# Hyena layer: low parts by accumulating transfers and VectorE in place of GpSimd, spectrum products in four wide operations

## The chip, the core and the metric

One core of a Trainium2 chip runs two transformer blocks over 256 positions of width 1024. The metric is the device time of one execution in microseconds. TensorE (PE; PEld is its weight load), VectorE (DVE), ScalarE (ACT), GpSimd (POOL) and SyncE (SP, which issues most transfers) each take their own instructions in order and wait for each other by semaphores.

## The reference

The whole program is a first block (stick-breaking attention, memory attention, an FFN), an MLA layer with a convolutional FFN, and a Hyena layer with a convolutional FFN. The change is in the Hyena layer:

```python
def hyena_mixer(x, w_in, w_short, ..., d_bias, w_o):
    u = dwconv_centred(x @ w_in, w_short)          # 256 x 3072
    v, g1, g2 = jnp.split(u, 3, axis=-1)
    filt = hyena_filters(length, ...)
    n = 2 * length
    z = v
    for o, gate in enumerate((g1, g2)):
        k_f = jnp.fft.rfft(two_sided_kernel(filt[:, o, 0], filt[:, o, 1]), n=n, axis=0)
        z_f = jnp.fft.rfft(z, n=n, axis=1)
        y = jnp.fft.irfft(z_f * k_f, n=n, axis=1)[:, :length]
        z = gate * (y + d_bias[o] * z)
    return z @ w_o
```

Around it stand a layer norm and the FFN `(silu(g) * a) @ w_down` with `a, g = split(dwconv(x @ w_up))`.

## The kernel before

Every product is made of three matmuls on numbers split in two: `hi` is the value rounded to the short format that TensorE takes at full rate, `lo` is the rest, and hi·hi + lo·hi + hi·lo is summed in PSUM. A weight comes in slabs of 128 x 1024 floats (512 KB). `weights` loads a slab into `wraw` (3 buffers, by SP), ScalarE rounds it to `whi`, and another engine makes `wlo = wraw - whi` (`whi` and `wlo` have 5 buffers each). TensorE then takes, for a projection (`gemm_b`), eight products with whi, eight with wlo and eight with whi against the low part of x.

`share["every"]` says which engine makes `wlo`: with 0 it is VectorE, with n every n-th slab goes to GpSimd. In the Hyena layer's input projection it is `HY_POOL = 1`, so all 20 slabs (called 4 to 23; the first four come in another form) go to GpSimd, and for the 8 slabs of its output projection it is `WO_POOL = 2`, so four of them do.

The Hyena layer runs on TensorE in one written order. `hy_mm(nt)` projects slab nt into a bank `hin` (4 banks, shared with the `y` of the inverse transforms); `dwconv` makes `u` or `g` of it in three operations (ScalarE, then VectorE lines 761 and 763), which frees the bank; `hy_time` transposes two u into `hyt`. The 1024 channels are worked in two halves, and each half has two orders, so there are four spectra:
- `spectrum` multiplies z by the DFT matrices (`X`: 12 matmuls), ScalarE copies one half (`ev`), VectorE adds and subtracts into `W`, and then the complex product with the filter's spectrum `Kf` is made in ten VectorE operations of 128 x 512 and two additions on GpSimd (lines 954 to 959). Tiles are `spec_w` and `spec_q`.
- `even_odd` or `both` splits the result into `yh`, `yl`; `back1` or `back2` transforms back on TensorE into `y` and multiplies by the gate.
- Between a spectrum and its inverse, TensorE has projections of later slabs to do. For the fourth spectrum these are the first four slabs of the output projection (`acc`).

A scheduler in the tile layer sets each engine's order from dependences and its own cost estimates, so that the code's order is kept only roughly on VectorE and ScalarE; the order after the change is read from the built program below.

Of the kernel before, what the change touches and what calls it, by code (L numbers as in the profile page):

```python
# [9 lines left out]
F32 = mybir.dt.float32  # L10
# [3 lines left out]
AF = mybir.ActivationFunctionType  # L14
ALU = mybir.AluOpType
# [19 lines left out]
PI_IN = 3.1415925  # L35
RAW_BUFS = 3
SPLIT_BUFS = 5
HY_POOL = 1
WO_POOL = 2
FF2_POOL = (0, 0)  # L40
WARM = 12
F4_TAGS = (("f4h0", "f4l0"), ("f4h1", "f4l1"))

# [2 lines left out]
def block_kernel(ctx, tc, A, out, taps=None):  # L46
    nc = tc.nc
# [17 lines left out]
        return [[acc_bank(b, h) for h in range(2)] for b in range(2)]  # L65


    def split(hi, lo, src, eng=nc.vector):
        nc.scalar.activation(hi, src, AF.Copy)  # L69
        eng.tensor_tensor(lo, src, hi.bitcast(F32), op=ALU.subtract)  # L70
# [4 lines left out]
    def raw_tile():  # L75
        return wraw.tile([P, 1024], F32, name="wraw", tag="wraw")

    share = {"every": 0, "n": 0}

    def weights(ap, dst=None):  # L80

        share["n"] += 1
        eng = nc.gpsimd if share["every"] and share["n"] % share["every"] == 0 else nc.vector
        n = ap.shape[-1]
        raw = raw_tile()
        hi, lo = dst or [wspl.tile([P, 1024], F32R, name=t, tag=t) for t in ("whi", "wlo")]
        norm["load"] = nc.sync.dma_start(raw[:, :n], ap)
        with ExitStack() as es:
            if norm["after"] > 0:
                norm["after"] -= 1  # L90
                es.enter_context(tc.issue_after(norm["inst"].ins))
            split(hi[:, :n], lo[:, :n], raw[:, :n], eng)
        return hi, lo

    def gemm_b(ps, w, off, x, kts):
# [108 lines left out]
    class Down:  # L204
# [4 lines left out]
        def __init__(self, total, tail=TAIL):  # L209
            self.acc, self.n, self.head, self.pend = None, 0, total - tail, []  # L210

        def add(self, act, wap):
            w = weights(wap)
            if self.acc is None:
                self.acc = acc_banks()
            if self.n >= self.head:
                self.pend.append((act, w))
            else:
                for b in range(2):
                    for h in range(2):  # L220
                        gemm_a(self.acc, b, h, act, w, self.n == 0, False)
            self.n += 1
# [261 lines left out]
    dn = Down(8)  # L484
# [29 lines left out]
    dn = Down(FF1_TILES)  # L514
# [137 lines left out]
    for i in range(2):  # L652
        w = weights(A["w_uq_r"][i])
# [83 lines left out]
    dn = Down(8)  # L737
# [30 lines left out]
    Kf = keep.tile([P, 2, 2, 2, D], F32, name="Kf")  # L768
# [71 lines left out]
    def conv_ffn(layer, x, utok, nxt, side):  # L840
        with ExitStack() as es:
            pf = es.enter_context(tc.tile_pool(name=f"pf{layer}", bufs=1))
            todo = side(es.enter_context(tc.tile_pool(name="flt", bufs=1))) if side else []
            per = -(-len(todo) // (FF2_TILES - 5))
            wc = lnp.tile([P, 2 * FF2_TILES, 3], F32, name="wc", tag="wc")
            nc.sync.dma_start(wc, A["ffn_w_conv"][layer])
            gb = ln_load(pf, A["ln2_g"][layer], A["ln2_b"][layer])
            dn = Down(FF2_TILES, TAIL if nxt is not None else SPLIT_BUFS)
            share["every"] = FF2_POOL[layer]

            def mm(nt):
                w = weights(A["ffn_w_up"][layer, nt])
                ps = bank("up")
                gemm_b(ps[:, :S], w, 0, x, KT)
                return ps[:, :S]

            def act(j, pss):
                ts = []
                for i in range(2):
                    t = pf.tile([P, S], F32, name=f"t{i}", tag=f"t{i}", bufs=2)  # L860
                    dwconv(t, pss[i], wc[:, j + i * FF2_TILES, :])
                    ts.append(t)
                ta, tg = ts
                nc.scalar.activation(tg, tg, AF.Silu)
                nc.vector.tensor_tensor(ta, ta, tg, op=ALU.mult)
                return act_split(pf, ta, "h", 5)

            def up(j):
                return act(j, [mm(2 * (j - 2) + i) for i in range(2)])

            ready = [up(2)]
            ready += [act(j, first_pair(utok, j)) for j in range(2)]
            order = [2, 0, 1] + list(range(3, FF2_TILES))
            for i in range(FF2_TILES):
                if i + 3 < FF2_TILES:
                    ready.append(up(i + 3))
                dn.add(ready[i], A["ffn_w_down"][layer, order[i]])
                if i:
                    for f, *a in todo[(i - 1) * per:i * per]:
                        f(*a)  # L880
            share["every"] = 0
            return dn.end(gb, ALPHA_2, nxt)

    x, utok = conv_ffn(0, x, utok, A["hy_w_in_f"], hyena_filter)
# [8 lines left out]
    g2 = p4.tile([P, KT, S], F32, name="g2", tag="g2")  # L893

    def hy_mm(nt):
        w = weights(A["hy_w_in"][nt - 4])
        ps = bank("hin")
        gemm_b(ps[:, :S], w, 0, x, KT)
        return ps[:, :S]
# [36 lines left out]
    def spectrum(o, c, z, own):  # L936

        cs = slice(c * 512, (c + 1) * 512)
        fh, fl = dft["c_fwd"]
        W = p4.tile([P, 2, 2, 512], F32, name="spec_w", tag="spec_w")  # L940
        Q = p4.tile([P, 2, 2, 512], F32, name="spec_q", tag="spec_q")
        for j in range(2):
            eo = []
            for b in range(2):
                ps = acc_bank(j, b, "X") if own else bank("X")
                mm3(ps, (fh[:, b, j], fl[:, b, j]), (z[0][:, b], z[1][:, b]), True, True)
                eo.append(ps)
            ev = p4.tile([P, 512], F32, name="ev", tag="ev", bufs=2)
            nc.scalar.activation(ev, eo[0], AF.Copy)
            for i, op in enumerate((ALU.add, ALU.subtract)):  # L950
                nc.vector.tensor_tensor(W[:, i, j], ev, eo[1], op=op)
        for i in range(2):
            kr, ki = Kf[:, o, i, 0, cs], Kf[:, o, i, 1, cs]
            nc.vector.tensor_tensor(Q[:, i, 0], W[:, i, 0], kr, op=ALU.mult)
            nc.vector.tensor_tensor(Q[:, i, 1], W[:, i, 1], ki, op=ALU.mult)  # L955
            nc.vector.tensor_tensor(Q[:, i, 0], Q[:, i, 0], Q[:, i, 1], op=ALU.subtract)  # L956
# [86 lines left out]
    z0 = back1(0, y)  # L1043
# [150 lines left out]
```

## Time and profile before

| | |
|---|---|
| median of 3 runs | 989.87 us (989.59, 989.87, 994.86) |
| the profiled execution | 988.41 us, its span 986.6 us |
| mean granted TensorE clock in it | 0.986 |
| TensorE, VectorE, ScalarE, GpSimd busy | 946.4, 760.4, 524.5, 123.3 us |
| Hyena layer, first slab's projection to the last inverse | 644.9 to 773.4 us |

A row of the profile's groups names line, engine, operation, output<-inputs, shape and count, then busy time and mean duration in ns, then the idle time before it and what ended that. A row of the timeline is start, length, engine, line and tiles; `xN` at its end merges N neighbours. A row of waits reads: who waited for whom, total us, times, longest. The granted clock (PEclk) is the share of full speed that TensorE was given.

### The profile page before, as it was taken

To read this page: it belongs to the slowest core of one execution; us is meant where nothing else is said; L and a number is where in the kernel's file an instruction comes from. 1 tells how busy PE (TensorE), PEld (TensorE's weight loads), DVE (VectorE), ACT (ScalarE), POOL (GpSimd) and SP (SyncE) were. 2 spreads that over 40 slices of the span, in tenths; PEclk is the share of its full clock that TensorE was granted. 3 is DMA by queue.
4 is the path that set the end of the run, shared out by engine and by line. 5 is a ranking of instruction groups with operands and counts; after the bars stand their busy time and mean duration, and the time that the engine had idled before them with its cause. 6 is when DMAs were issued, how large, how long until landed. Compare 5 with 4: busy or idle time off the path is not lost.

```text
span 986.6 us, 15543 instructions
## 1 busy us (share of the span) xinstructions
PE 946.4 (96%) x6020; PEld 841.1 (85%) x6020; DVE 760.4 (77%) x1177; ACT 524.5 (53%) x859; POOL 123.3 (12%) x78
## 2 busy tenths in 40 slices
PE   9999999999999999999999999998879899999996
PEld 7889789888998888888899999788867789999995
DVE  6776678666557777779889887869998778777776
ACT  5676526445445576556666665345453346555551
POOL 0000000000000110011311211177453000000000
PEclk9999999999999999999999999999999899999999
DMA  7744436656565543466545556443222455555551
GB/s 242 278 170 129 154 122 221 178 190 179 183 192 187 173 128 107 149 244 210 196 164 184 171 170 220 132 160 106 98 86 86 171 192 193 179 185 185 181 191 43
DMA packets 48921, 165.97 MB, mean 168 GB/s; under 512 B 5995, under 2 KB 6860, under 8 KB 48720
## 3 DMA queue, kind: packets, MB, share of 16 engines
q1 hardware_dynamic: 48656, 164.34, 50.5%
q8 instruction: 47, 0.77, 0.3%
q0 software_dynamic: 192, 0.66, 0.2%
q14 instruction: 26, 0.21, 0.1%
HBM read 163.27 MB, written 1.05 MB: 167 GB/s over the span
## 4 chain that ended last, share of the span: by engine, by line
PE 76%; DVE 13%; DMA 5%; ACT 3%; issue 2%; POOL 0%; SPq 0%; DVEq 0%; ACTq 0%
PE up L102 30%; PE acc L108 8%; PE acc L107 8%; PE acc L109 8%; PE f L189 5%; PE proj L102 2%; DVE wlo L70 2%; PE z L107 1%; DMA wraw<-w_qk 1%; DVE yl L70 1%; DVE spec_q L956 1%; ACT whi L69 1%; DVE spec_q L955 1%; PE qn L102 1%; DMA wraw<-w_v 1%
## 5 line engine op out<-in xcount | busy, mean ns | idle before, releaser
L70 DVE TENSOR_TENSOR wlo<-wraw,whi 128x1024 fp32r<-128x1024 f32 (+1 forms) x246 | 300.6, 1225 | 71.2 <-ACT whi L69 70.9
L69 ACT ACTIVATE whi<-wraw 128x1024 fp32r<-128x1024 f32 (+1 forms) x270 | 281.0, 1045 | 113.3 <-PE acc L108 54.3
L102 PE MATMUL up<-xh,whi 128*128 128x256 f32 x864 | 122.0, 283 | 1.3 <-DVE t L763 1.3
L102 PEld LDWEIGHTS up<-xh,whi 128*128 128x128 f32 x864 | 115.3, 191 | 8.3 <-ACT whi L69 1.6
L102 PE MATMUL up<-xh,wlo 128*128 128x256 f32 x864 | 121.3, 283 | 0.0
L102 PE MATMUL up<-xl,whi 128*128 128x256 f32 x864 | 121.3, 283 | 0.0
L108 PE MATMUL acc<-whi,hl 128*128 128x512 f32 x304 | 119.6, 394 | 1.5 <-DVE hl L70 1.5
L109 PE MATMUL acc<-wlo,hh 128*128 128x512 f32 x304 | 119.6, 395 | 0.0
L107 PE MATMUL acc<-whi,hh 128*128 128x512 f32 x304 | 119.3, 394 | 0.0
L102 PEld LDWEIGHTS up<-xl,whi 128*128 128x128 f32 x864 | 111.5, 192 | 0.0
L102 PEld LDWEIGHTS up<-xh,wlo 128*128 128x128 f32 x864 | 111.4, 192 | 0.0
L156 POOL TENSOR_TENSOR ln_rs<-ln_rs,mhalf 128x1 f32<-128x1 f32 x12 | 11.7, 971 | 629.1 <-DVE ln_rs L155 629.1
L760 ACT ACTIVATE t<-up,wc 128x256 f32<-128x256 f32 x80 | 37.8, 474 | 94.8 <-PE up L102 94.7
L761 DVE SCALAR_TENSOR_TENSOR t<-up,wc,t 128x255 f32<-128x255 f32 x80 | 38.2, 479 | 51.4 <-ACT t L760 51.3
L108 PEld LDWEIGHTS acc<-whi,hl 128*128 128x128 f32 x304 | 57.1, 188 | 12.9 <-DVE hl L70 2.5
L109 PEld LDWEIGHTS acc<-wlo,hh 128*128 128x128 f32 x304 | 57.1, 188 | 12.7
L107 PEld LDWEIGHTS acc<-whi,hh 128*128 128x128 f32 x304 | 57.6, 189 | 10.9 <-ACT hh L69 0.6
L70 POOL TENSOR_TENSOR wlo<-wraw,whi 128x1024 fp32r<-128x1024 f32 x24 | 59.5, 2497 | 54.8 <-ACT whi L69 54.7
L763 DVE SCALAR_TENSOR_TENSOR t<-up,wc,t 128x255 f32<-128x255 f32 x80 | 38.3, 480 | 2.1
L524 ACT ACTIVATE h<-up 128x256 f32<-128x256 f32 x28 | 10.8, 385 | 54.7 <-PE up L102 51.5
L525 DVE TENSOR_TENSOR h<-h 128x256 f32<-128x256 f32 x32 | 13.5, 424 | 27.0 <-ACT h L524 26.4
L829 POOL TENSOR_TENSOR Kf<-f_eo 128x512 f32<-128x512 f32 x16 | 23.0, 1460 | 63.5 <-ACT f_eo L826 63.5
(411 smaller groups left out, 1684.6 us busy)
## 6 DMA issues: line engine op xcount, KB each, us to landing
wraw<-ffn_w_up SPq DMA_DIRECT2D x80, 512.0 KB, 3.5
wraw<-ffn_w_down SPq DMA_DIRECT2D x44, 512.0 KB, 3.5
wraw<-w_down SPq DMA_DIRECT2D x32, 512.0 KB, 3.7
wraw<-w_up SPq DMA_DIRECT2D x28, 512.0 KB, 3.6
wraw<-hy_w_in SPq DMA_DIRECT2D x20, 512.0 KB, 3.3
wraw<-w_qk SPq DMA_DIRECT2D x14, 512.0 KB, 4.6
wraw<-w_out SPq DMA_DIRECT2D x8, 512.0 KB, 3.5
wraw<-mla_w_o SPq DMA_DIRECT2D x8, 512.0 KB, 3.3
```

Of the source, the lines that this page charges most:

```text
L69: nc.scalar.activation(hi, src, AF.Copy)
L70: eng.tensor_tensor(lo, src, hi.bitcast(F32), op=ALU.subtract)
L102: nc.tensor.matmul(ps, a[:, off + k * P:off + (k + 1) * P], m[:, k, :], start=i == 0, stop=i == len(seq) - 1)
L107: nc.tensor.matmul(ps, ah, mh, start=start, stop=False)
L108: nc.tensor.matmul(ps, al, mh, start=False, stop=False)
L109: nc.tensor.matmul(ps, ah, ml, start=False, stop=stop)
L189: nc.tensor.matmul(ps, x[xi][:, k, tb], ws[k // 2][wi][:, o:o + 512], start=i == 0, stop=i == len(seq) - 1)
L525: nc.vector.tensor_tensor(h, h, h, op=ALU.mult)
L760: norm["act"] = nc.scalar.activation(dst, ps, AF.Copy, scale=w3[:, 1:2])
L761: nc.vector.scalar_tensor_tensor(dst[:, 1:], ps[:, :S - 1], w3[:, 0:1], dst[:, 1:], op0=ALU.mult, op1=ALU.add)
L763: norm["dve"] = nc.vector.scalar_tensor_tensor(dst[:, :S - 1], ps[:, 1:S], w3[:, 2:3], dst[:, :S - 1], op0=ALU.mult, op1=ALU.add)
L829: nc.gpsimd.tensor_tensor(Kf[:, o, i, j, cs], eo[0], eo[1], op=op)
```

## The change

Three things. (1) 17 of the layer's 28 slabs (w_in 9 to 23; w_o 0 and 2) get their low part so: ScalarE writes -whi into wlo, and a transfer issued by GpSimd reads the slab from memory a second time and adds it in. (2) The other 11 low parts (w_in 4 to 8; w_o 1, 3, 4 to 7) are made by VectorE. (3) The complex product is four VectorE operations, two over 2048 and two over 1024 elements per partition; GpSimd does none of it. `FF2_POOL` was (0, 0), so its removal changes nothing.

```diff
-HY_POOL = 1
-WO_POOL = 2
-FF2_POOL = (0, 0)
+HY_DMA = range(9, 24)
+WO_DMA = (0, 2)
...
-    def weights(ap, dst=None):
-
-        share["n"] += 1
-        eng = nc.gpsimd if share["every"] and share["n"] % share["every"] == 0 else nc.vector
+    def weights(ap, dst=None, dma=False):
...
         norm["load"] = nc.sync.dma_start(raw[:, :n], ap)
+        if dma:
+            nc.scalar.activation(hi[:, :n], raw[:, :n], AF.Copy)
+            nc.scalar.activation(lo[:, :n], raw[:, :n], AF.Copy, scale=-1.0)
+            nc.gpsimd.dma_start(lo[:, :n], ap, accum_op=ALU.add)
+            return hi, lo
...
     def hy_mm(nt):
-        w = weights(A["hy_w_in"][nt - 4])
+        w = weights(A["hy_w_in"][nt - 4], dma=nt in HY_DMA)
...
-        for i in range(2):
-            kr, ki = Kf[:, o, i, 0, cs], Kf[:, o, i, 1, cs]
-            nc.vector.tensor_tensor(Q[:, i, 0], W[:, i, 0], kr, op=ALU.mult)
-            nc.vector.tensor_tensor(Q[:, i, 1], W[:, i, 1], ki, op=ALU.mult)
-            nc.vector.tensor_tensor(Q[:, i, 0], Q[:, i, 0], Q[:, i, 1], op=ALU.subtract)
-            nc.vector.tensor_tensor(W[:, i, 0], W[:, i, 0], ki, op=ALU.mult)
-            nc.vector.tensor_tensor(W[:, i, 1], W[:, i, 1], kr, op=ALU.mult)
-            nc.gpsimd.tensor_tensor(W[:, i, 0], W[:, i, 0], W[:, i, 1], op=ALU.add)
+        kf = Kf[:, o, :, :, cs]
+        nc.vector.tensor_tensor(Q, W, kf, op=ALU.mult)
+        nc.vector.tensor_tensor(Q[:, :, 0], Q[:, :, 0], Q[:, :, 1], op=ALU.subtract)
+        nc.vector.tensor_tensor(W, W, kf[:, :, ::-1], op=ALU.mult)
+        nc.vector.tensor_tensor(W[:, :, 0], W[:, :, 0], W[:, :, 1], op=ALU.add)
...
-        dn.add((z0[0][:, k, :], z0[1][:, k, :]), A["hy_w_o"][k])
+        dn.add((z0[0][:, k, :], z0[1][:, k, :]), A["hy_w_o"][k], k in WO_DMA)
```

The order also moves. On VectorE, in the first spectrum, the kernel before runs its second half like this (u_7351 and u_7357 come from slabs 8 and 9):

```order
L954 TENSOR_TENSOR spec_q_7159<-spec_w_7158,Kf_4541 128x512
L955 TENSOR_TENSOR spec_q_7159<-spec_w_7158,Kf_4541 128x512
L957 TENSOR_TENSOR spec_w_7158<-spec_w_7158,Kf_4541 128x512
L956 TENSOR_TENSOR spec_q_7159<-spec_q_7159 128x512
L958 TENSOR_TENSOR spec_w_7158<-spec_w_7158,Kf_4541 128x512
L70 TENSOR_TENSOR zl_6993<-hyt10_7196,zh_6992 128x2x256
L70 TENSOR_TENSOR zl_6993<-hyt11_7273,zh_6992 128x2x256
L761 SCALAR_TENSOR_TENSOR u_7351<-hin_7217,ws_6986,u_7351 128x255
L761 SCALAR_TENSOR_TENSOR u_7357<-hin_7248,ws_6986,u_7357 128x255
L763 SCALAR_TENSOR_TENSOR u_7351<-hin_7217,ws_6986,u_7351 128x255
L763 SCALAR_TENSOR_TENSOR u_7357<-hin_7248,ws_6986,u_7357 128x255
```

After the change the same place on VectorE reads (u_7267 and u_7273 are slabs 6 and 7, u_7346 is slab 8):

```order
L950 TENSOR_TENSOR spec_w_7158<-ev_7180,X11_7176 128x512 x2
L69 TENSOR_TENSOR zl_6993<-hyt10_7188,zh_6992 128x2x256
L952 TENSOR_TENSOR spec_q_7159<-spec_w_7158,Kf_4541 128x2048
L764 SCALAR_TENSOR_TENSOR u_7267<-hin_7087,ws_6986,u_7267 128x255
L953 TENSOR_TENSOR spec_q_7159<-spec_q_7159 128x2x512
L954 TENSOR_TENSOR spec_w_7158<-spec_w_7158,Kf_4541 128x2048
L762 SCALAR_TENSOR_TENSOR u_7273<-hin_7133,ws_6986,u_7273 128x255
L955 TENSOR_TENSOR spec_w_7158<-spec_w_7158 128x2x512
L764 SCALAR_TENSOR_TENSOR u_7273<-hin_7133,ws_6986,u_7273 128x255
L762 SCALAR_TENSOR_TENSOR u_7346<-hin_7209,ws_6986,u_7346 128x255
```

The u of slabs 6 and 7 were finished ahead of the first spectrum and now end between and behind its wide operations; TensorE transposes the u of slab 7 before it projects slab 11.

On ScalarE, ahead of and in the first spectrum, the kernel before has (whi_7289 is slab 10, u_7280 slab 7):

```order
L69 ACTIVATE whi_7289<-wraw_7288 128x1024
L760 ACTIVATE u_7197<-hin_7000,ws_6986 128x256
L760 ACTIVATE u_7203<-hin_7041,ws_6986 128x256
L760 ACTIVATE u_7274<-hin_7087,ws_6986 128x256
L69 ACTIVATE whi_7320<-wraw_7319 128x1024
L760 ACTIVATE u_7280<-hin_7133,ws_6986 128x256
L69 ACTIVATE whi_7379<-wraw_7378 128x1024
L949 ACTIVATE ev_7168<-X00_7160 128x512
L949 ACTIVATE ev_7180<-X10_7172 128x512
L69 ACTIVATE zh_6992<-hyt10_7196 128x2x256
```

After the change it has (wlo_7236, wlo_7283 and wlo_7315 are the negated copies of slabs 9, 10 and 11, each followed by its transfer on GpSimd):

```order
L761 ACTIVATE u_7267<-hin_7087,ws_6986 128x256
L86 ACTIVATE wlo_7236<-wraw_7234 128x1024
L761 ACTIVATE u_7273<-hin_7133,ws_6986 128x256
L948 ACTIVATE ev_7168<-X00_7160 128x512
L86 ACTIVATE wlo_7283<-wraw_7281 128x1024
L948 ACTIVATE ev_7180<-X10_7172 128x512
L68 ACTIVATE zh_6992<-hyt10_7188 128x2x256
L85 ACTIVATE whi_7314<-wraw_7313 128x1024
L86 ACTIVATE wlo_7315<-wraw_7313 128x1024
```

The copy of slab 10 stands between the two ev, and the rounding of slab 11 has moved behind them, with its copy after it.

On VectorE in the fourth spectrum the order is now as follows (the wlo are slabs 5, 6 and 7 of w_o; before the change one of w_o's low parts stood there):

```order
L952 TENSOR_TENSOR spec_q_8026<-spec_w_8025,Kf_4541 128x2048
L69 TENSOR_TENSOR wlo_8225<-wraw_8223,whi_8224 128x1024
L953 TENSOR_TENSOR spec_q_8026<-spec_q_8026 128x2x512
L954 TENSOR_TENSOR spec_w_8025<-spec_w_8025,Kf_4541 128x2048
L69 TENSOR_TENSOR yl_8134<-spec_q_8026,yh_8133 128x512
L955 TENSOR_TENSOR spec_w_8025<-spec_w_8025 128x2x512
L69 TENSOR_TENSOR yl_8134<-spec_q_8026,yh_8133 128x512
L69 TENSOR_TENSOR wlo_8231<-wraw_8229,whi_8230 128x1024
L69 TENSOR_TENSOR yl_8134<-spec_w_8025,yh_8133 128x512 x2
L69 TENSOR_TENSOR wlo_8237<-wraw_8235,whi_8236 128x1024
```

Low parts of the output projection stand between the spectrum's operations and ahead of the last yl. TensorE's own order differs only in where some transposes and a few products of y stand. SP's order is the same.

More of the change, by code (lines that the diff above doesn't have):

```diff
@@ L65, in acc_banks, with split @@
         return [[acc_bank(b, h) for h in range(2)] for b in range(2)]
-    def split(hi, lo, src, eng=nc.vector):
+    def split(hi, lo, src):
         nc.scalar.activation(hi, src, AF.Copy)
-        eng.tensor_tensor(lo, src, hi.bitcast(F32), op=ALU.subtract)
+        nc.vector.tensor_tensor(lo, src, hi.bitcast(F32), op=ALU.subtract)
     norm = {"inst": None, "after": 0}
@@ L76, in raw_tile @@
         return wraw.tile([P, 1024], F32, name="wraw", tag="wraw")
-    share = {"every": 0, "n": 0}
-    def weights(ap, dst=None):
-        share["n"] += 1
-        eng = nc.gpsimd if share["every"] and share["n"] % share["every"] == 0 else nc.vector
+    def weights(ap, dst=None, dma=False):
         n = ap.shape[-1]
@@ L91, in weights @@
                 es.enter_context(tc.issue_after(norm["inst"].ins))
-            split(hi[:, :n], lo[:, :n], raw[:, :n], eng)
+            split(hi[:, :n], lo[:, :n], raw[:, :n])
         return hi, lo
@@ L210, in __init__, with add @@
             self.acc, self.n, self.head, self.pend = None, 0, total - tail, []
-        def add(self, act, wap):
-            w = weights(wap)
+        def add(self, act, wap, dma=False):
+            w = weights(wap, dma=dma)
             if self.acc is None:
@@ L848, in conv_ffn @@
             dn = Down(FF2_TILES, TAIL if nxt is not None else SPLIT_BUFS)
-            share["every"] = FF2_POOL[layer]
             def mm(nt):
@@ L880, in conv_ffn @@
                         f(*a)
-            share["every"] = 0
             return dn.end(gb, ALPHA_2, nxt)
@@ L1022, in back2 @@
         return nz
-    share["every"] = HY_POOL
     z0, z1 = new_z(), new_z()
@@ L1061, in block_kernel @@
     s1 = spectrum(1, 1, z1, False)
-    share["every"] = WO_POOL
     dn = Down(8)
     for k in range(4):
-        dn.add((z0[0][:, k, :], z0[1][:, k, :]), A["hy_w_o"][k])
+        dn.add((z0[0][:, k, :], z0[1][:, k, :]), A["hy_w_o"][k], k in WO_DMA)
     y = both(*s1)
@@ L1070, in block_kernel @@
         dn.add((z1[0][:, k - 4, :], z1[1][:, k - 4, :]), A["hy_w_o"][k])
-    share["every"] = 0
     x, utok = dn.end(gb, ALPHA_2, A["ffn_w_up_f"][1], spare(p4, (("yh", "yl"), ("g1", "g2"))))
```

## The prediction

> **What bounds the kernel now.** I read the page first: where is TensorE not busy at full clock?
>
> ```profile
> span 986.6 us, 15543 instructions
> PE 946.4 (96%) x6020; PEld 841.1 (85%) x6020; DVE 760.4 (77%) x1177; ACT 524.5 (53%) x859; POOL 123.3 (12%) x78
> POOL 0000000000000110011311211177453000000000
> PEclk9999999999999999999999999999999899999999
> ```
>
> TensorE sets the time nearly everywhere. The one stretch that differs is the Hyena layer, where GpSimd is dense and the clock dips. So next, the windows view of that stretch (the columns are the stretch, its length, then busy time and instruction count per engine, granted clock, DMA share). It is cut at the places where TensorE passes from projections to spectra and back.
>
> ```profile
> core 0: us, PE busy (x) PEld busy (x) DVE busy (x) ACT busy (x) POOL busy (x), PEclk, DMA share, GB/s
> 644.80:661.40 16.60, 16.35 (x124) 15.40 (x123) 10.76 (x24) 9.50 (x14) 16.44 (x7) 1.00 0.54 182
> 661.40:686.30 24.90, 21.07 (x160) 20.56 (x159) 24.69 (x34) 11.51 (x20) 15.74 (x8) 0.93 0.33 112
> 686.30:691.90 5.60, 5.60 (x27) 4.65 (x26) 4.35 (x7) 3.17 (x6) 4.82 (x3) 1.00 0.58 187
> 691.90:716.10 24.20, 20.29 (x153) 19.80 (x151) 24.08 (x31) 11.27 (x19) 11.66 (x6) 0.93 0.25 87
> 716.10:721.70 5.60, 5.54 (x24) 4.62 (x25) 5.53 (x9) 2.24 (x5) 3.55 (x2) 1.00 0.43 144
> 721.70:739.20 17.50, 11.68 (x97) 11.47 (x95) 17.38 (x24) 9.38 (x15) 7.44 (x4) 0.92 0.22 75
> 739.20:749.50 10.30, 10.23 (x60) 9.81 (x61) 7.77 (x17) 2.50 (x6) 1.12 (x1) 0.81 0.44 147
> 749.50:760.70 11.20, 11.20 (x50) 9.02 (x49) 11.20 (x15) 4.28 (x7) 4.11 (x2) 1.00 0.15 53
> 760.70:773.40 12.70, 8.52 (x50) 7.50 (x49) 9.13 (x11) 2.84 (x6) 4.42 (x2) 0.73 0.44 164
> sum 128.60, PE 110.47 PEld 102.83 DVE 114.88 ACT 56.69 POOL 69.30; mean PE 12.27 PEld 11.43 DVE 12.76 ACT 6.30 POOL 7.70
> ```
>
> In the four spectrum stretches (661, 692, 722, 750) VectorE is full. TensorE is idle for 128.60 - 110.47 = 18.1 us. After a wait the clock is low: busy time times (1 - clock), summed over rows two, four, six, seven and nine, is 1.5 + 1.4 + 0.9 + 1.9 + 2.3 = 8.1 us. So 26.2 us of the stretch are lost, and 102.4 us is its floor. TensorE's waits there name VectorE:
>
> ```profile
> PE hyt L910 <- DVE u L763: 7.0, 2, 3.6
> PE y L107 <- DVE g L763: 5.9, 1, 5.9
> PE y L108 <- DVE yl L70: 4.2, 4, 2.1
> ```
>
> Why is VectorE late? The groups by shape, and the timeline of the first wait:
>
> ```profile
> L956 DVE TENSOR_TENSOR spec_q<-spec_q 128x512 f32<-128x512 f32 x8 | 12.1, 1510 | 0.0
> L955 DVE TENSOR_TENSOR spec_q<-spec_w,Kf 128x512 f32<-128x512 f32 x8 | 11.0, 1371 | 0.0
> L954 DVE TENSOR_TENSOR spec_q<-spec_w,Kf 128x512 f32<-128x512 f32 x8 | 5.5, 683 | 0.0
> L70 POOL TENSOR_TENSOR wlo<-wraw,whi 128x1024 fp32r<-128x1024 f32 x24 | 59.5, 2497 | 54.8 <-ACT whi L69 54.7
> ```
>
> ```profile
> 671.59 2.85 POOL L70 TENSOR_TENSOR wlo<-wraw,whi 128x1024 fp32r<-128x1024 f32 x1
> 672.10 2.89 DVE L956 TENSOR_TENSOR spec_q<-spec_q 128x512 f32<-128x512 f32 x1
> 677.50 0.86 DVE L763 SCALAR_TENSOR_TENSOR u<-hin,ws,u 128x255 f32<-128x255 f32 x2
> 678.11 1.06 PE L910 MATMUL hyt<-ident,u 128*128 128x128 f32 x4 [3.41 <-DVE u L763]
> 678.83 2.05 PE L102 MATMUL hin<-xh,whi 128*128 128x256 f32 x8
> 683.08 1.12 PE L102 MATMUL hin<-xh,whi 128*128 128x256 f32 x8
> 684.04 1.12 PE L102 MATMUL hin<-xh,wlo 128*128 128x256 f32 x8
> ```
>
> The same 512-wide work takes 683 ns at L954 and 1510 ns at L956. The 2.89 us one starts inside a GpSimd split and ends with it (674.4 and 675.0). It pushes the u that TensorE's transposes wait for, 3.41 us, and the next eight projection products then take 2.05 instead of 1.12 us. L956 and L955 alone carry 8 x (1510 - 683) + 8 x (1371 - 683) = 12.1 us of such excess.
>
> **The change, part by part.** Prices first:
>
> ```profile
> 630.34 2.35 DVE L70 TENSOR_TENSOR wlo<-wraw,whi 128x1024 fp32r<-128x1024 f32 x2
> 675.52 1.28 DVE L70 TENSOR_TENSOR zl<-hyt,zh 128x512 fp32r<-128x512 f32 x2
> 660.97 1.06 ACT L949 ACTIVATE ev<-X 128x512 f32<-128x512 f32 x2
> L69 ACT ACTIVATE whi<-wraw 128x1024 fp32r<-128x1024 f32 x27 | 28.4, 1055 | 14.2 <-PE f L189 3.8 <-DMA wraw<-hy_w_in 3.6 <-DVE u L758 3.5
> L758 DVE TENSOR_SCALAR u<-f4t,ws 128x256 f32<-128x256 f32 x4 | 1.8, 476 | 7.6 <-PE f4t L199 7.6
> 639.23 1.42 DVE L70 TENSOR_TENSOR xl<-ln_t,xh 128x512 fp32r<-128x512 f32 x2 [0.72 <-ACT xh L69]
> 643.05 1.98 PE L189 MATMUL f<-whi,xl 128*128 128x512 f32 x8
> L661 POOL DMA_DIRECT2D rope_sw<-rope_in x4: 492/518/682, 344.4 to 347.3; - x4
> DMA to landing us min/median/max: 4.4/5.2/5.4
> wraw<-hy_w_in SPq DMA_DIRECT2D x20, 512.0 KB, 3.3
> q1 hardware_dynamic: 48656, 164.34, 50.5%
> ```
>
> *GpSimd's 24 splits and 8 adds go.* That returns VectorE's excess; the 18.1 us of waits and 8.1 us of slow clock are what can come back, and no more.
>
> *Spectrum.* Back to back, 512 wide costs 1.28 - 0.68 = 0.60 us and 1024 wide 2.35 - 1.22 = 1.13 us, so 2048 wide is 1.13 + 1024 x (1.13 - 0.60)/512 = 2.19 us, an estimate (at most 4 x 0.60 = 2.40). Ten undisturbed operations cost 6.0 us; now 2 x 2.19 + 2 x 1.13 = 6.64, so 0.64 more for each of four spectra, and the first half is ready only with the second.
>
> *Seven more low parts on VectorE* (11 against 4), 7 x 1.13 = 7.9 us. Those of the first four slabs fall into the 7.6 us in which VectorE waits for f4t, so nothing; without that cover they would delay the first u by up to 4.5 us. One of them stands in the order ahead of the layer norm's two xl: those end at 640.65 and are wanted at 643.05, 2.4 us later, more than 1.13. The fifth lies ahead of the first spectrum, and three of the last four between its operations in the last one.
>
> *Seventeen negated copies on ScalarE*, 17 x 1.055 = 17.9 us. In this stretch it goes from 56.7 of 128.6 to about 75 of 109 us, so it is no bound. In the order one copy stands between the two ev of the first spectrum: VectorE has 1.2 us of additions in that time, so some 0.3 us. SP's loads now wait for that copy instead of GpSimd's 2.5 us split, so they come no later.
>
> *Seventeen accumulating transfers.* Issuing one costs GpSimd 0.5 to 0.7 us by L661; only they stand in its queue until the next layer norm. Two things count: landing and throughput. I follow the new order from 661. Slabs 10 and 11 are tightest: their copies end near 662.6 (one copy behind the first ev, which ends at 661.5) and 665.8 (then ev, zh, whi and a copy), and TensorE wants the low parts 0.96 us into their projections (2.88 us each, from 684.04 - 683.08), at 669.2 and 672.5, so 6.6 us of room each. A landing between 3.3 us (a plain load of that size) and 5.4 (the slowest rope_sw) fits.
> Throughput: q1 moved 164.34 MB in 0.505 x 986.6 = 498 us of all engines, so 512 KB hold them 1.6 us. An accumulating one costs between 1.6 and, by four rope_sw of 160 KB issued from 344.4 and landed by 347.3 + 5.4 = 352.7, 79 GB/s or 6.6 us. I take 2.3, nearer the load, which has the same size and rows, with something for also reading the destination. Then 15 slabs of w_in, each with one load and one accumulation, need 15 x 3.9 = 59 us between 657 and 721, where 64 are there; with queueing 1 us of waits.
> The Trainium skill ("Collectives: The Full Stack", section "The bandwidth ceiling: the fold count and why AG ≠ RS ≠ AR") says that an addition in the transfer path costs twice the reads of a copy; no trace here shows it. By it the price would be 3.2 us, and 15 x 4.8 = 72 us would overrun the 64 by 8.
>
> *What is late next*, with undisturbed prices along VectorE's new order:
> - First spectrum: additions from 661.6, then zl, the wide product, u, difference, second product, u, sum, u: 2.5 + 0.6 + 2.2 + 0.4 + 1.1 + 2.2 + 0.4 + 1.1 + 0.4 = 10.9, so 672.5. TensorE reaches the transposes of that u at 671.0, three projections and two groups of transposes (0.5 each) after 661.4. Wait 1.5, and 0.3 later at hyt or y.
> - Second: a u more and no other work ahead, so the u's needed are done 11.1 us after the additions begin; TensorE needs four projections and 0.6, 12.1. No wait.
> - Third: the u after which the bank is free that y waited 5.9 us for is done some 10.5 us after the additions begin; TensorE arrives after four projections, 11.5. yl leaves 0.5.
> - Fourth: TensorE covers it with 11.2 us of acc, VectorE needs 4 additions, 6.6, four yl and three low parts, 14.9 from 1 us earlier. Wait 2.7, plus 1.0 for the clock.
>
> Sum: 26.2 - 1.8 - 0.5 - 3.7 - 1.0 (transfers) = 19.2 us gained. The profiled execution took 988.41 us, 1.5 below the median 989.87 of the three; 969.2 on its scale, 970.7 on that of the median. I say **971**. Nothing outside the Hyena layer moves.
>
> **The rivals.**
> 1. *Transfers are the new bound, mildly.* If each holds the engines like two loads, 2 x 1.6 = 3.2 us, 15 x 4.8 = 72 us overrun the 64 by 8, of which 1 is counted: 978. For it: the destination is read too. Against: DMA share there is only 0.22 to 0.58.
> 2. *Transfers are the bound, badly: slower.* From about 4.0 us each (15 x 5.6 = 84 us, 20 more than there are) the gain is eaten; at 4.8, thrice the load, 15 x 6.4 = 96 us, 32 too many: 1002. For it: the rope_sw bound. Against: those are short rows over 32 partitions, and four latencies in a row.
> 3. *VectorE stays late.* Wide operations hold the chain, its new order puts low parts inside spectra. If each of four waits keeps 3 us with its clock loss of 1: 16 lost instead of 6, 980. For it: VectorE still has some 95 us of work in 109.
> 4. *VectorE holds up the issue of transfers.* Each would wait for the longest VectorE operation, 2.2 us: landing near 8, over the 6.6 us of room at slabs 10 and 11, 2 us once: 973. The Trainium skill ("SBUF — State Buffer", section "Who interferes with whom") says that a GpSimd-issued transfer starves for descriptors behind a VectorE operation in a two-port mode, and that tensor_tensor has no such mode; by it this rival would follow only for VectorE's other operations. No row here shows a hold: rope_sw's issues took 492 to 682 ns.
> 5. *Nothing gained*: GpSimd was not the cause, 988. The 2.89 us rows speak against it.
>
> **How the numbers follow.** Chances: forecast 0.46 (964 to 975), rival 4 0.08, rival 1 0.18, rival 3 0.14, rival 2 0.10, rival 5 0.04. Under 0.5% (4.9 us) no measurement of this kernel tells a change from none, so faster means below 985: forecast, 4, 1, 3 and little else, 0.85; same 0.05; slower 0.10. The floor gives 989.9 - 26.2 = 964; I take 963 as the low end, and 985 as the high one, which holds rivals 1, 3 and 4 with some growth and leaves out rivals 2 and 5.
>
> **What would show it.** GpSimd rows in this stretch are transfers only. The spectrum products take one price without 2.9 us outliers, near 2.2 us at 2048 wide. The two waits of hyt for u shrink from 7.0 to under 2.5, y for g (5.9) vanishes, y for yl stays near 3, and the granted clock is 0.97 or more. Wrong if: TensorE's products with wlo wait for a transfer (landing over 7 us), the DMA share there is above 0.9, or VectorE operations still double in length beside GpSimd's issues.

## The result, and the profile after

The changed kernel takes 974.72 us (median; 972.63 to 977.33), the kernel before 989.73 beside it. The ratio is 0.983, 95% interval 0.980 to 0.985: 15.0 us gained; the forecast was a time of 971 us. The profiled execution took 974.68 us. Its page, with the rows that answer to those of before:

```profile
span 972.9 us, 15529 instructions
PE 942.5 (97%) x6020; PEld 840.2 (86%) x6020; DVE 741.8 (76%) x1160; ACT 540.2 (56%) x876; POOL 67.2 (7%) x63
POOL 0000000000000110002213111002210000000000
DMA  8843437656556461637565555448994565555551
```

GpSimd's dense part is gone. In its place three of the forty slices of the DMA engines read 8 or 9, where little else in the second half of the run is above 6. TensorE's two ends of the stretch that the prediction cut out, from the timeline (start, length, what):

```profile
648.36 1.12 PE L103 MATMUL hin<-xh,whi 128*128 128x256 f32 x8
760.12 0.39 PE L108 MATMUL acc<-whi,zh 128*128 128x512 f32 x1
```

The stretch takes 760.12 - 648.36 = 111.76 us against 128.6: 16.8 us gained of the 26.2 that were lost in it. It begins 3.5 us later than in the profile of before, but all that lies ahead of the change: over the fourteen executions profiled for this study it began between 644.9 and 649.3. So below each kernel has its stretch (first `hin` product to the first `acc` product of the output projection's last four slabs) beside its time, from one profiled execution each.

TensorE's waits there, and VectorE's groups by shape:

```profile
PE hyt L909 <- DVE u L764: 2.9, 1, 2.9
PE hin L103 <- DMA wlo<-hy_w_in: 2.0, 1, 2.0
PE y L108 <- DVE g L764: 0.8, 2, 0.6
PE y L109 <- DVE yl L69: 0.4, 1, 0.4
```

```profile
L952 DVE TENSOR_TENSOR spec_q<-spec_w,Kf 128x2048 f32<-128x2048 f32 x4 | 9.2, 2288 | 0.0
L953 DVE TENSOR_TENSOR spec_q<-spec_q 128x1024 f32<-128x1024 f32 x4 | 4.9, 1217 | 0.0
```

No operation of VectorE is stretched any more, and the 5.9 us wait of y for g is 0.8. A wait for a transfer is new. The windows view (stretch, length, busy time per engine, granted clock, DMA share, GB/s) says where:

```profile
core 0: us, PE busy (x) PEld busy (x) DVE busy (x) ACT busy (x) POOL busy (x), PEclk, DMA share, GB/s
656.00:668.00 12.00, 12.00 (x92) 11.51 (x91) 11.11 (x19) 8.29 (x13) 1.81 (x2) 1.00 0.59 131
668.00:680.00 12.00, 10.00 (x72) 9.80 (x71) 7.77 (x10) 7.10 (x9) 3.07 (x4) 0.86 1.05 285
680.00:692.00 12.00, 9.10 (x63) 8.92 (x62) 8.15 (x16) 9.63 (x14) 2.13 (x3) 0.86 1.06 265
692.00:704.00 12.00, 12.00 (x80) 11.01 (x79) 9.81 (x14) 9.35 (x15) 2.86 (x4) 1.00 1.02 261
704.00:716.00 12.00, 12.00 (x101) 11.96 (x100) 11.81 (x20) 10.93 (x16) 2.37 (x3) 1.00 1.01 258
```

From 668 on the DMA engines are full (a share of 1.0), and TensorE loses nearly all that it still loses in the first 24 us of that: 24 - 19.1 = 4.9 us idle and 19.1 x 0.14 = 2.7 us by the clock. How, the timeline of that place shows:

```profile
664.24 0.88 POOL L87 DMA_DIRECT2D wlo<-hy_w_in  x1 [3.17 <-ACT wlo L86]
673.85 1.21 PE L103 MATMUL hin<-xh,wlo 128*128 128x256 f32 x8 [2.00 <-DMA wlo<-hy_w_in]
680.97 1.06 ACT L85 ACTIVATE whi<-wraw 128x1024 fp32r<-128x1024 f32 x1 [1.38 <-DMA wraw<-hy_w_in]
681.93 0.58 ACT L68 ACTIVATE zh<-hyt 128x512 fp32r<-128x512 f32 x1
682.54 0.69 DVE L69 TENSOR_TENSOR zl<-hyt,zh 128x512 fp32r<-128x512 f32 x1 [6.77 <-ACT zh L68]
683.15 0.47 DVE L764 SCALAR_TENSOR_TENSOR u<-hin,ws,u 128x255 f32<-128x255 f32 x1
683.77 0.48 PE L909 MATMUL hyt<-ident,u 128*128 128x128 f32 x2 [2.90 <-DVE u L764]
```

Slab 10's transfer (its projection is the seventh from 648.36), issued at 664.24, lands 9.6 us later and 2.0 us too late. Then a chain that no row of it names as a DMA wait of TensorE: ScalarE waits for a slab's load, its zh stands behind that slab's whi, VectorE's zl waits for zh (6.77 us idle), the u behind zl in VectorE's queue is late, and TensorE waits 2.90 us for that u. The DMA issues (size, median us to landing) and queues (packets, MB, share of 16 engines):

```profile
wraw<-hy_w_in SPq DMA_DIRECT2D x20, 512.0 KB, 8.1
wlo<-hy_w_in POOLq DMA_DIRECT2D x15, 512.0 KB, 8.8
q1 hardware_dynamic: 48656, 164.34, 52.0%
q0 software_dynamic: 2640, 9.57, 5.0%
```

The loads take 8.1 us instead of 3.3. The queue of the 17 transfers held the engines for (5.0% - 0.2%) x 972.9 = 46.7 us, 2.7 us each.

### The profile page after: what moved, and what is told of

It is laid out like the page before. It is cut to its first block, busy times and chain, and to the rows that moved or that the text cites. A ratio compares the mean times of both kernels' runs of the same rounds, so it can differ in the third digit from the quotient of the medians.

```text
span 972.9 us, 15529 instructions
## 1 busy us (share of the span) xinstructions
PE 942.5 (97%) x6020; PEld 840.2 (86%) x6020; DVE 741.8 (76%) x1160; ACT 540.2 (56%) x876; POOL 67.2 (7%) x63
## 3 DMA queue, kind: packets, MB, share of 16 engines
q1 hardware_dynamic: 48656, 164.34, 52.0%
## 4 chain that ended last, share of the span: by engine, by line
PE 84%; DVE 7%; DMA 5%; ACT 3%; issue 1%; POOL 0%; DVEq 0%; SPq 0%; POOLq 0%; ACTq 0%
PE up L103 31%; PE acc L108 9%; PE acc L109 9%; PE acc L110 9%; PE f L190 5%; PE proj L103 4%; PE hin L103 2%; DMA wraw<-hy_w_in 2%; PE z L108 1%; DVE wlo L69 1%; PE qn L103 1%; DMA wraw<-hy_w_o 1%; PE o L734 1%; PE z L109 1%; PE ln_t L170 1%
## 5 line engine op out<-in xcount | busy, mean ns | idle before, releaser
L69 DVE TENSOR_TENSOR wlo<-wraw,whi 128x1024 fp32r<-128x1024 f32 (+1 forms) x253 | 307.0, 1216 | 75.4 <-ACT whi L68 75.2
L68 ACT ACTIVATE whi<-wraw 128x1024 fp32r<-128x1024 f32 (+1 forms) x253 | 263.1, 1044 | 110.6 <-PE acc L109 53.1
L103 PE MATMUL up<-xh,wlo 128*128 128x256 f32 x864 | 121.3, 283 | 0.0
L103 PE MATMUL up<-xl,whi 128*128 128x256 f32 x864 | 121.3, 283 | 0.0
L103 PEld LDWEIGHTS up<-xl,whi 128*128 128x128 f32 x864 | 111.4, 192 | 0.0
L103 PEld LDWEIGHTS up<-xh,wlo 128*128 128x128 f32 x864 | 111.4, 192 | 0.0
L103 PE MATMUL hin<-xh,wlo 128*128 128x256 f32 x160 | 23.1, 288 | 2.0 <-DMA wlo<-hy_w_in 2.0
```

The costliest lines, as they stand in the source:

```text
L69: nc.vector.tensor_tensor(lo, src, hi.bitcast(F32), op=ALU.subtract)
L103: nc.tensor.matmul(ps, a[:, off + k * P:off + (k + 1) * P], m[:, k, :], start=i == 0, stop=i == len(seq) - 1)
```

## The experiments

Theory after the result: GpSimd's work at VectorE's side stretched VectorE's operations, and its removal is the gain; what is missing to the full 26 us goes to the transfers, which fill the DMA engines. Rivals: the wide operations are the gain; GpSimd's results were waited for; the rest is VectorE's own. e4, e5 and e9 leave out low parts or halves of them, so they do not compute the layer; they only price a part. All in one table, ratios to the kernel before on the same chip, stretches as above:

| kernel | median us | ratio to before, 95% | stretch us |
|---|---|---|---|
| before / changed | 989.73 / 974.72 | 0.983 (0.980 to 0.985) | 128.6 / 111.8 |
| e1_wide | 990.30 | 0.998 (0.996 to 1.000) | 125.9 |
| e2_narrow | 983.03 | 0.989 (0.987 to 0.991) | 115.1 |
| e3_allvec | 985.26 | 0.992 (0.989 to 0.996) | 122.9 |
| e4_notransfer | 966.04 | 0.972 (0.969 to 0.975) | 103.5 |
| e5_busy | 976.16 | 0.983 (0.980 to 0.987) | 114.1 |
| e6_narrowvec | 978.42 | 0.987 (0.983 to 0.991) | 111.8 |
| e7_sbuf | 985.70 | 0.994 (0.992 to 0.996) | 125.6 |
| e8_third | 986.59 | 0.994 (0.992 to 0.997) | 121.3 |
| e9_halfbytes | 965.98 | 0.975 (0.972 to 0.977) | 105.5 |
| e10_from10 | 974.10 | 0.981 (0.978 to 0.985) | 111.4 |
| e11_from5 | 976.48 | 0.985 (0.982 to 0.987) | 114.8 |
| e12_quarter | 975.04 | 0.983 (0.981 to 0.986) | 111.0 |

### What stretched VectorE

**e1_wide**: the kernel before with the new `spectrum` alone (the cut shows its beginning).

```diff
-        for i in range(2):
-            kr, ki = Kf[:, o, i, 0, cs], Kf[:, o, i, 1, cs]
...
+        kf = Kf[:, o, :, :, cs]
+        nc.vector.tensor_tensor(Q, W, kf, op=ALU.mult)
...
```

> The kernel before with the four wide operations alone; GpSimd keeps its 24 splits. Theory (GpSimd's splits stretch VectorE's operations, and taking them away is the gain): the wide operations are stretched just so, rows of 3 us and more instead of 2.3, and VectorE gets GpSimd's eight additions as well: 986 to 994 us. Rival (the width of the operations is the gain): 980 or less.

As the theory had it, next to nothing: GpSimd's splits stretch the wide operations instead (VectorE's groups; 2.29 and 1.22 us in the changed kernel). In this stretch only SP's loads wait for GpSimd, and ScalarE's rounding waits 3.5 us in all for those loads; still 125.9 - 102.4 = 23.5 us are lost.

```profile
L955 DVE TENSOR_TENSOR spec_w<-spec_w,Kf 128x2048 f32<-128x2048 f32 x4 | 13.6, 3389 | 0.0
L954 DVE TENSOR_TENSOR spec_q<-spec_q 128x1024 f32<-128x1024 f32 x4 | 13.2, 3309 | 0.0
```

**e2_narrow** and **e6_narrowvec**: the changed kernel with the ten narrow operations back. In e2 the two additions of a spectrum are on GpSimd as before, in e6 on VectorE. This is the one line in which the two differ:

```diff
-            nc.gpsimd.tensor_tensor(W[:, i, 0], W[:, i, 0], W[:, i, 1], op=ALU.add)   # e2
+            nc.vector.tensor_tensor(W[:, i, 0], W[:, i, 0], W[:, i, 1], op=ALU.add)   # e6
```

> The changed kernel with the narrow spectrum of before (ten operations of 512 on VectorE, two additions on GpSimd). Theory: no splits, so the 512-wide rows take 0.69 us and little changes: 972 to 979 us, the most by which GpSimd's eight additions stretch VectorE. Rival (width is the gain): 984 or more.

> The changed kernel with the narrow products of before, twelve operations of 512 all on VectorE; against e2_narrow only the two additions a spectrum move from GpSimd to VectorE. Theory (in e2_narrow the eight GpSimd additions of 1.53 us did the harm; their neighbours took 1.24 and 0.95 us instead of 0.69): 12 x 0.69 = 8.2 us a spectrum against 7.0 wide, 974 to 979 us. Rival (the width is worth the 8 us between 983 and 974.7): 981 to 985.

e2 lay above my range. Its groups show the eight additions and the VectorE operations that stand beside them, 1240 instead of 684 ns:

```profile
L954 DVE TENSOR_TENSOR spec_q<-spec_w,Kf 128x512 f32<-128x512 f32 x8 | 9.9, 1240 | 0.0
L958 POOL TENSOR_TENSOR spec_w<-spec_w 128x512 f32<-128x512 f32 x8 | 12.3, 1534 | 31.9 <-DVE spec_w L957 31.9
```

In e6 all narrow operations take 0.69 us, and its stretch is 111.8 us, that of the changed kernel. So width by itself is worth nothing that shows there; moving the additions off GpSimd is worth 115.1 - 111.8 = 3.3 us. A part of that may be waiting and not stretching: ScalarE's `yh` waits 5.1 us for these additions in e2, as it did for 5.6 us in the kernel before:

```profile
ACT yh L69 <- POOL spec_w L959: 5.6, 4, 2.1
```

e6's median is 3.7 us above the changed kernel's with overlapping intervals. Behind the stretch both narrow kernels are longer in their profiles, 217.1 us (e2) and 218.1 (e6) against 212.8, in waits of the last slabs, the next layer norm and the FFN. Why, I did not try, so it is not shown that width is worth nothing over the whole kernel.

**e5_busy**: no transfers (as e4 below), and for each of 15 slabs two GpSimd subtractions that nobody waits for.

```diff
-            nc.gpsimd.dma_start(lo[:, :n], ap, accum_op=ALU.add)
+            if idle is not None:
+                for h in (hi[:, :512], hi[:, 512:]):
+                    nc.gpsimd.tensor_tensor(idle, h.bitcast(F32), h.bitcast(F32), op=ALU.subtract)
...
```

> The changed kernel without its 17 transfers (966.0 us), and for each of the 15 slabs of w_in that had one, GpSimd subtracts whi from itself in two operations of 128 x 512 into a tile that nobody reads. Nothing waits for GpSimd. Theory (GpSimd's work at the side stretches VectorE's operations, and that alone made the kernel before late): 30 x 1.3 = 40 us of such work against 59.5 us before, which cost up to 26 us: about two thirds, 978 to 986 us, with VectorE rows far above 0.69 and 2.29 us. Rival (what was lost before was waiting for GpSimd's results): 964 to 968.

10.1 us above e4, somewhat under my range. No row of its trace waits for these subtractions, so waiting for GpSimd's results is not what makes its work dear here. It does not show that the 5.6 us of `yh` above cost nothing in the kernel before. Groups of VectorE and GpSimd:

```profile
L957 DVE TENSOR_TENSOR spec_w<-spec_w,Kf 128x2048 f32<-128x2048 f32 x4 | 10.8, 2707 | 0.0
L89 POOL TENSOR_TENSOR idle<-whi 128x512 f32<-128x512 f32 x30 | 43.2, 1441 | 38.0 <-ACT whi L85 19.9 <-DMA wraw<-hy_w_in 16.1
```

Which operations are stretched, the timeline of e1 shows best:

```profile
657.83 7.18 POOL L70 TENSOR_TENSOR wlo<-wraw,whi 128x1024 fp32r<-128x1024 f32 x3
662.60 2.48 DVE L951 TENSOR_TENSOR spec_w<-ev,X 128x512 f32<-128x512 f32 x4
671.03 2.86 POOL L70 TENSOR_TENSOR wlo<-wraw,whi 128x1024 fp32r<-128x1024 f32 x1 [0.49 <-ACT whi L69]
671.54 4.50 DVE L955 TENSOR_TENSOR spec_w<-spec_w,Kf 128x2048 f32<-128x2048 f32 x1
```

Four additions of ev and X run beside GpSimd's splits and take 2.48 us together, their usual 0.68 us each (they overlap a little), while a product of spec_w with Kf takes 4.50 us. X lies in PSUM, spec_w and Kf both in SBUF. The Trainium skill ("SBUF — State Buffer", section "Who interferes with whom") says that a VectorE instruction with two SBUF inputs contends with a GpSimd instruction that reads SBUF, and that one with at most one SBUF input, outside the two-port modes, does not. These rows agree with it in both halves.

The product does not run slowly, it stands still: the split ends 2.35 us after the product's start, and 2.15 us later the product is done, near its 2.28 us undisturbed. The one that begins first is not held: in e5 a product that began 0.45 us ahead of a subtraction took 2.28 us, and the subtraction 2.73 us where the quickest took 1.04.

### What the transfers cost

**e4_notransfer**: the accumulating transfers left out.

```diff
-            nc.gpsimd.dma_start(lo[:, :n], ap, accum_op=ALU.add)
```

> The changed kernel with the 17 accumulating transfers left out, so that the low part stays the negated rounded slab... more exactly the negated slab that ScalarE wrote, and the output is not the layer's; all else stands. It prices the transfers. Theory (they slow the loads from 3.3 to 8 us, ScalarE's queue then waits for loads, and one low part lands late): the 2.0 us and 2.9 us waits and the slow clock behind them go: 968 to 972 us. Rival (the transfers are hidden, and VectorE's late operations keep the rest): 974 to 976.

They cost 974.7 - 966.0 = 8.7 us (stretch: 8.3), more than I had expected from the waits; 966.04 us lies below my range. Without them the stretch is 103.5 us, 1.1 above the 102.4 that the prediction gave as its floor; the loads land in 3.2 us, and TensorE is nearly whole at full clock where it lost most:

```profile
668.00:680.00 12.00, 11.13 (x93) 10.93 (x93) 11.57 (x18) 11.93 (x18) 0.00 (x0) 1.00 0.66 220
680.00:692.00 12.00, 12.00 (x81) 11.02 (x80) 10.32 (x20) 9.36 (x14) 0.00 (x0) 1.00 0.42 133
```

**e9_halfbytes**: each transfer with half the columns; same instructions and waits.

```diff
-            nc.gpsimd.dma_start(lo[:, :n], ap, accum_op=ALU.add)
+            nc.gpsimd.dma_start(lo[:, :n // 2], ap[:, :n // 2], accum_op=ALU.add)
```

> The changed kernel with each of the 17 transfers accumulating only the first 512 of the slab's 1024 columns, so that the second half of each low part stays the negated slab. The same instructions, queues and waits; only the bytes of the transfers halve. Between 966.0 us without transfers and 974.7 with them: theory (the DMA engines are full, and what counts is by how much they are over): 17 x 1.4 = 23 us less in a stretch that has some 60 us at a share of 1.0, so the share falls below 0.85 and nearly all comes back, 966 to 968.5 us. Rival (each transfer costs by its presence, its issue and its landing): half or less comes back, 970 to 975.

965.98 us: by the median half the bytes give all of it back, by the stretch 6.3 of the 8.3 us. So most of it is neither the number of transfers nor ScalarE's second copy nor GpSimd's issue (872 ns each in the changed kernel, 863 to 934, with no sign of a hold by VectorE). What counts is how much the transfers move, and so how long they hold the DMA engines: 1.6 us each here by the queue's share ((3.0% - 0.2%) x 964.3 us / 17) instead of 2.7. Loads land in 4.2 us. My expectation of a share below 0.85 was wrong: the windows show the engines full for 12 us, and at 0.89 in the next. So a share near 1 is not by itself a loss.

```profile
668.00:680.00 12.00, 10.86 (x89) 10.50 (x88) 10.06 (x15) 9.77 (x14) 4.33 (x5) 1.00 1.04 276
680.00:692.00 12.00, 10.89 (x69) 9.66 (x68) 9.57 (x19) 10.04 (x16) 1.75 (x2) 1.00 0.89 221
```

**e7_sbuf**: the raw slab on the chip as the transfer's source.

```diff
-            nc.gpsimd.dma_start(lo[:, :n], ap, accum_op=ALU.add)
+            nc.gpsimd.dma_start(lo[:, :n], raw[:, :n], accum_op=ALU.add)
```

> The changed kernel with wraw, already on the chip, as the source of the accumulating transfers in place of the slab in memory. wraw is then held until the transfer has landed. Theory (what a transfer holds the engines for is set by its own elements and the destination's): the time of 16 engines for a transfer stays 2.7 us, the DMA share stays near 1, and with loads issued later 975 to 985 us. Rival (the second read from memory is what costs): the share of the transfers' queue falls from 5.0% to 3.5% or less, and 967 to 972 us.

985.70 us is just above my range. The transfers' queue takes as much as with memory for a source, and SP now waits for the transfers before it can load again:

```profile
q0 software_dynamic: 2640, 9.57, 5.3%
SPq L83 <- DMA wlo<-wraw: 73.8, 17, 7.2
```

So the second read from memory is not what makes them dear, and a source in memory has an advantage of its own: it frees the raw buffer.

### Who should make the low parts

**e3_allvec** and **e8_third**: no transfers, and two thirds of those of w_in.

```diff
-HY_DMA = range(9, 24)
-WO_DMA = (0, 2)
+HY_DMA = ()                                              # e3
+WO_DMA = ()                                              # e3
+HY_DMA = [n for n in range(9, 24) if n % 3 != 1]         # e8
```

> The changed kernel without accumulating transfers: all 28 low parts on VectorE. Theory: no contention and no second read, but VectorE gets 17 x 1.22 = 20.7 us more in a stretch of 112 us in which it is busy for 97, so it is the bound there: 979 to 987 us. Rival (the transfers cost more than VectorE's operations would): 974 or less.

> The changed kernel with every third of the 15 w_in transfers (slabs 10, 13, 16, 19, 22) given back to VectorE: 12 transfers. Theory (the DMA engines are full from 668 to 728 us, the loads come late, ScalarE waits for them and VectorE and TensorE behind it): 5 x 2.75 = 14 us of DMA time go for 5 x 1.22 = 6.1 us of VectorE, which is idle for some 15 of 112 us; loads land in 5 to 6 us instead of 8.1, 968 to 973 us. Rival (VectorE is as tight as the DMA engines): 975 to 980.

e3 came as expected; between 655 and 745 us SP waits 87.9 us there for VectorE's low parts, and TensorE's projections 4.4 us. e8 did not: fewer transfers, fewer bytes, and 12 us slower than the changed kernel. SP's waits between 655 and 745 us point at the cause, with a wait of TensorE below; the first row is of the changed kernel, the others of e8_third:

```profile
SPq L83 <- DVE wlo L69: 2.1, 1, 2.1
```

```profile
SPq L83 <- DVE wlo L69: 23.9, 6, 8.3
PE hin L103 <- DMA wlo<-hy_w_in: 5.9, 4, 2.9
```

SP waits for some raw buffer in either kernel; what counts is when it comes free. A low part given to VectorE stands in its queue behind a whole spectrum, holds one of three raw buffers meanwhile, and the next loads wait. Slab 10 is the first: its buffer comes free at 676.4 us, when VectorE has made its low part, and the load that takes it is issued then; in the changed kernel ScalarE frees it at 663.9 us. The slabs behind it are late, with their transfers: slab loads arrive in bursts, two transfers are issued back to back, and TensorE waits four times for one. My price of 1.22 us for a low part on VectorE was that of the operation, not of what it holds.

**e10_from10** and **e11_from5**: one transfer fewer, and four more, at the front.

```diff
-HY_DMA = range(9, 24)
+HY_DMA = range(10, 24)     # e10
+HY_DMA = range(5, 24)      # e11
```

> The changed kernel with slab 9 given back to VectorE, whose low part then stands ahead of the first spectrum's additions; slabs 10 to 23 keep their transfers. Theory (DMA engines full from slab 9 on, slab 11 waits 2.0 us for its transfer): one transfer of 2.75 us less ahead of slab 11 takes that wait away, 1.2 us of VectorE are added ahead of the first spectrum: 971 to 975 us. Rival (a low part on VectorE costs more by what it holds up, as in e8_third): 976 to 980.

> The changed kernel with four more transfers, slabs 5 to 23: VectorE makes none of their low parts but slab 4's. Theory (DMA engines full): the stretch ahead of slab 9 has a DMA share of 0.5 to 0.6, so four more transfers of 2.75 us, 11 us, fit into its 10 spare us but for a little, and the first spectrum starts with the engines full: 974 to 979 us. Rival (VectorE ahead of the first spectrum is what makes it late; it loses 4 x 1.2 us of work): 968 to 972.

Both lie in the theory's ranges and within the spread of the changed kernel. But these ranges hold the changed kernel's own 974.7 us too, so the times only speak against the rivals. The slab that waited 2.0 us is slab 10 by the count of the projections, not 11 as e10's expectation has it; in e10 products with wlo still wait 1.3 us for transfers, so the wait that should go stays in part, and its stretch is the changed kernel's within 0.3 us. In e11 the loss only moves forward: its windows show the engines full, and TensorE short, 12 us earlier.

```profile
656.00:668.00 12.00, 9.20 (x49) 7.34 (x47) 4.40 (x10) 8.53 (x11) 3.46 (x4) 0.86 0.93 257
668.00:680.00 12.00, 7.06 (x45) 7.06 (x46) 7.63 (x10) 6.31 (x9) 1.74 (x2) 0.72 0.99 255
```

**e12_quarter**: an attempt to beat both. The transfer takes 768 columns, GpSimd subtracts the other 256.

```diff
-            nc.scalar.activation(lo[:, :n], raw[:, :n], AF.Copy, scale=-1.0)
-            nc.gpsimd.dma_start(lo[:, :n], ap, accum_op=ALU.add)
+            m = 3 * n // 4
+            nc.scalar.activation(lo[:, :m], raw[:, :m], AF.Copy, scale=-1.0)
+            nc.gpsimd.tensor_tensor(lo[:, m:n], raw[:, m:n], hi[:, m:n].bitcast(F32),
+                                    op=ALU.subtract)
+            nc.gpsimd.dma_start(lo[:, :m], ap[:, :m], accum_op=ALU.add)
```

> The changed kernel with each transferred slab's low part shared: ScalarE's copy and the accumulating transfer take 768 columns, and GpSimd subtracts the other 256 (nothing left out). Theory (two costs, each with its own price): a transfer of three quarters holds the engines for 2.1 us, between the half that cost nothing (966.0 us) and the whole that cost 8.7, say 2; GpSimd's 17 x 0.7 = 12 us of subtractions against the 43 us that cost 10 in e5_busy, 2.8 us: 969 to 972.5 us, faster than the changed kernel's 974.7. Rival (any GpSimd work beside VectorE falls where TensorE waits, and 768 columns still fill the DMA engines): 974 to 979.

975.04 us, no better. Both costs are there again: GpSimd's 256 columns took 740 ns in the median, near the 0.7 us I had put down, but 1016 ns in the mean and up to 2494; VectorE's 1024-wide sums took 1427 instead of 1217 ns, and the DMA engines are still full where it matters.

```profile
L88 POOL TENSOR_TENSOR wlo<-wraw,whi 128x256 fp32r<-128x256 f32 x17 | 17.3, 1016 | 40.4 <-ACT whi L85 40.3
L958 DVE TENSOR_TENSOR spec_w<-spec_w 128x1024 f32<-128x1024 f32 x4 | 5.7, 1427 | 0.0
668.00:680.00 12.00, 7.58 (x57) 7.22 (x56) 7.67 (x12) 7.74 (x12) 7.11 (x8) 0.91 1.02 267
```

No version that computes the layer beat the changed kernel measurably.

## Why the prediction was right, and where it was not

The mechanism of the gain was right: GpSimd's work caused the loss, and taking it away is the gain. That the time came within 0.4% of the forecast is in part luck, for two of its terms were wrong in opposite directions, by 4.9 and 7.3 us. The forecast left 7.0 us of loss in the stretch: 6.0 for VectorE's lateness and 1.0 for the transfers. Measured, the loss is 111.8 - 102.4 = 9.4 us: 1.1 (e4: 103.5 - 102.4) and 8.3.

- *GpSimd's work is the cause of the loss.* Shown: e1 keeps its splits and 23.5 of the 26.2 us of loss, e5 puts 43.2 us of such work back without any dependence and loses 10.1 us, e4 without it reaches the floor within 1.1 us. How much of the loss was stretching and how much waiting for its additions is not separated.
- *The prices of VectorE's operations.* 2.19 and 1.13 us back to back were right: in the fourth spectrum VectorE starts a 2048-wide product at 749.77 and the next operation at 751.97, 2.20 us later, and 1024-wide operations follow at 1.14. Single rows read 2.29 and 1.22 us because neighbours overlap a little.
- *What is late next* (1.5 + 0.3, 0, 0.5 and 2.7 + 1.0 us at the four spectra). Mis-sized: 1.1 us in all without the transfers. At the fourth spectrum, where 3.7 us were put down, VectorE's chain was right: from the first addition (741.43) to the end of the last yl (756.74) it took 15.3 us, forecast 14.9. But TensorE did not wait for its end. It began the inverse at 753.71 with the yl that were there, and waited 0.4 us for a later one.
- *Seven more low parts on VectorE cost nothing, seventeen copies on ScalarE are no bound.* e4 has them all and is within 1.1 us of the floor, so this stands.
- *SP's loads come no later.* This failed. It looked at when the raw buffer comes free and not at what shares the engines: 3.3 became 8.1 us.
- *Landing between 3.3 and 5.4 us, with 6.6 us of room at slabs 10 and 11.* It failed by its upper end: 6.6 at the least, 8.8 in the median. The place was right: slab 10 waited 2.0 us. The issue, put at 0.5 to 0.7 us, took 0.87.
- *2.3 us of the engines for a transfer, hence 1.0 us of waits.* 2.7 us measured, and 8.3 us lost. With 2.7 the sum is 15 x 4.3 = 64.5 us against 64, so the engines are full with nothing to spare. And it was an average over the whole stretch: TensorE takes slabs in runs of four to six, 2.88 us each, while a slab with its transfer holds the engines for 1.6 + 2.7 = 4.3 us: within a run the engines must fall behind, by that estimate, however much room the whole stretch has. Moreover 2.9 of TensorE's 4.9 us of idle time there came through ScalarE's and VectorE's queues, which the step did not follow.
- *The Trainium skill's rule on additions in the path* ("Collectives: The Full Stack", section "The bandwidth ceiling: the fold count and why AG ≠ RS ≠ AR"), twice the reads and by that 3.2 us, an estimate from the load here: the measured 2.7 us lies about midway between my 2.3 and that.
- *The rivals.* Rival 1's mechanism, the transfers as a mild bound, is what happened, though it did not end at its 978, since VectorE's part was smaller. Two of the three signs named for being wrong came true: a product with wlo waited for a transfer, and the DMA share went above 0.9. Rival 4, a hold of the issue, is out: 863 to 934 ns.
- *The signs.* Outliers gone, y for g down from 5.9 to 0.8, hyt for u 2.9 instead of under 2.5, y for yl 0.4 instead of near 3, clock 0.989 over the run but 0.86 in the 24 us where the engines fill.

From 692 to 716 the engines are still full, and it costs TensorE nothing (its rows there read 12.00 of 12.00). The transfers' landings say why. Slab 9's landed at 668.3, 0.2 us before TensorE took its wlo, so slab 10's, 5.5 us behind it, came too late for a TensorE that takes a slab in 2.88 us. Slab 14's landed at 689.0, and TensorE, held up and then busy with an inverse and a spectrum, came to its wlo only at 698.4: 9.3 us of lead. By slab 19 (landed 707.5, taken at 713.7) 6.3 us of it were left. What stays open is why the narrow kernels are longer behind the stretch, and how a split of the loss before into stretching and waiting would come out.

## What to carry to other kernels

An engine that nobody waits for can still set the time, by holding up another engine's operations: look for the same operation at two durations, and for which operands it has when it is slow. Before work is moved from an engine to transfers, sum what the DMA engines must do against the fastest run of consumption and not against the average, see how far ahead the first transfer is issued, and halve the bytes to see whether their fullness is the cost. And price work moved into an in-order queue by what it holds while it stands there: e8's 1.2 us operations cost more than the transfers that they replaced.

## What the runs showed of the hardware

- An accumulating transfer of 512 KB held the 16 engines for 2.7 us, a plain load of that size for 1.6 us (164.34 MB in 498 us, the kernel before). Half an accumulating transfer still took 1.6 us (e9). From SBUF instead of memory it was no cheaper (5.3% against 5.0% of the span for 17).
- It took GpSimd 0.87 us to issue one at each size tried (medians of 872 ns at 512 KB and at 256 KB, 883 at 384 KB), at most 0.96 us beside VectorE.
- GpSimd's subtraction of a low part took 740 ns for 256 columns (e12) and 2407 for 1024 (before) in the median, and up to 2494 and 2933 where VectorE was in the way.
- VectorE's operations with both inputs in SBUF stood still until a GpSimd subtraction that had begun before them ended: 4.50 us for a product of 2.28 (e1). Additions with one input in PSUM did not (at most 690 ns for all 16 in e1, four of them beside splits).
